# One-hots of the expert gate matrix laid out token by token, their matmuls one step later

## The chip, the cores and the metric

The kernel runs on one core of a Trainium2 chip. Its engines work side by side, each through its own list of instructions in order: TensorE (PE, with PEld for the loads of its stationary operand), VectorE (DVE), ScalarE (ACT), GpSimd (POOL) and SyncE (SP), which issues most of the DMAs. The metric is the device time of one execution in microseconds (us). Over three runs of the kernel before it was 1341.74 to 1342.67, with a median of 1341.83.

## What is computed

The reference is two transformer blocks over 256 tokens of width 1024: a block with window attention, retention and a gated feed-forward, then a block with a gated mixer, banded attention and a "PEER" feed-forward. The change lies in the PEER part, cut here to its core:

```python
q = (xb @ w_query).reshape(T, 8, 2, 128)
sc = jnp.einsum('thpd,hpkd->thpk', q, sub_keys)        # 8 heads, 2 halves, 128 keys each
s_top, i_top = lax.top_k(sc, 16)
cand = s_top[:, :, 0, :, None] + s_top[:, :, 1, None, :]
best, pos = lax.top_k(cand.reshape(T, 8, 256), 16)     # 16 experts of 128*128 per head
g = jax.nn.softmax(best, axis=-1)
h = jax.nn.gelu(jnp.einsum('thkd,td->thk', expert_u[eidx], xb))
out = jnp.einsum('thk,thkd->td', g * h, expert_v[eidx])
```

Each token so chooses 8 x 16 = 128 experts, each named by two numbers below 128, with a gate weight each.

## The kernel before, in words

The kernel gathers no experts. It computes the first layer for all 16384 of them, multiplies by a gate matrix that is zero where an expert was not chosen, and runs the whole second layer.

Every large product is made in fp32r from two parts of each operand (`hi`, a rounded copy, and `lo`, the rest): `mm3` (L105) issues three matmuls for each block of 128 along the sum, at L107, L108 and L109. A **unit** (L76) is one weight block of 128 x 1024: a DMA of 512 KB (L89), the copy to `whi` on ACT (L94) and the subtraction to `wlo` on DVE (L95). Units are given priority, so that they are issued some 80 instructions ahead of where the program stands; beyond that, the order on each engine is that of the program. There are three buffers for `whi` and `wlo` in this part of the kernel.

The first layer runs over j = 0 to 127 (L945). Each j takes one unit of `peer_u` and 24 matmuls of 256 columns (L926). After an odd j, the two results are passed through gelu into S, a matrix of 128 x 128 experts x 256 tokens (L932 to L936). Early in the loop DVE finds the top 16s and decodes the expert numbers; from then on `combine` (L851 to L879) is called after each odd j, about twice, until all 256 tokens are done near j = 115.

One call of `combine` makes the gate matrices of four tokens. The 128 chosen experts of a token lie along the partitions. A and B are one-hots of the experts' two numbers, and G0 and G1 are B times the gate's high and low half; all are fp16. The gate matrix of a token is then the product of A and G0 plus that of A and G1, 128 x 128 each, summed in PSUM (C). Its columns are one matmul each: eight matmuls of 128 columns for four tokens (L872), with a load of the stationary operand before each. DVE then multiplies S by C where S is already there (L875), and ACT copies C into the rest of S (L878).

A, B, G0 and G1 are stored as 128 numbers x 4 tokens with the token innermost. So DVE makes each for four tokens in one instruction of 512 elements (L861, L867, L868), and ACT makes G0 in four instructions, one for each token, since the gate is a factor per partition (L865). What a matmul reads for one token are 128 fp16 values that lie 8 bytes apart.

After the loop the second layer runs over 128 units of `peer_v` with 12 matmuls of 512 columns each (L974).

Of the kernel before, what the change touches and what calls it, by code (L numbers as in the profile page):

```python
# [7 lines left out]
F32 = mybir.dt.float32  # L8
F32R = mybir.dt.float32r
F16 = mybir.dt.float16  # L10
I32 = mybir.dt.int32
U32 = mybir.dt.uint32
AF = mybir.ActivationFunctionType
# [9 lines left out]
GP = 115  # L23
# [5 lines left out]
T = 256  # L29
# [13 lines left out]
class Net:  # L43
# [68 lines left out]
        return hl[0][:, k, ts], hl[1][:, k, ts]  # L112

    def gemm_t(self, ps, src, hl, K, k0=0, first=True, last=True, parts=None, engine=None):
        """ps[n, t] += W[k, n] x[k, t] for one unit of up to 8 k."""
        hi, lo = parts or self.unit(src, K * 128, engine=engine)
        for k in range(K):
            s = slice(k * 128, k * 128 + 128)
            self.mm3(ps, (hi[:, s], lo[:, s]), self.acts(hl, k0 + k),
                     first and k == 0, last and k == K - 1)  # L120
# [5 lines left out]
            self.mm3(ps, (hi[:, s], lo[:, s]), self.acts(hl, k), first and k == ks[0], last and k == ks[-1])  # L126

    def gemm_t_late(self, jobs, hl):
        """gemm_t of several (ps, src), with the last k after all others."""
        parts = [self.unit(src, 1024) for _, src in jobs]  # L130
        for (ps, _), w in zip(jobs, parts):
            self.gemm_k(ps, w, hl, range(7), first=True)
        for (ps, _), w in zip(jobs, parts):
            self.gemm_k(ps, w, hl, [7], last=True)

    def gemm_n(self, src, hl):
        """two banks, one per 128 tokens, of [t, 512] for a chunk of 512 columns."""
        banks = [self.mm_bank() for _ in range(2)]
        for q in range(4):
            hi, lo = self.unit(src[q], 1024)  # L140
            for tb in range(2):
                for k in range(2):
                    s = slice(k * 512, k * 512 + 512)
                    self.mm3(banks[tb], self.acts(hl, 2 * q + k, slice(tb * 128, tb * 128 + 128)),
                             (hi[:, s], lo[:, s]), q == 0 and k == 0, q == 3 and k == 1)
        return banks
# [8 lines left out]
            nc.vector.scalar_tensor_tensor(lo, src, scale, hi.bitcast(F32), op0=OP.mult, op1=OP.subtract)  # L155

    def rsqrt(self, y, ss, n, scale, pool=None):
        """y = (ss * scale + eps)^-1/2, all [128, n]."""
        nc = self.nc
        pool = pool or self.tiny  # L160
        v = pool.tile([128, n], F32, tag="nv", name="nv")
        nc.vector.tensor_scalar(v, ss, scale, EPS, op0=OP.mult, op1=OP.add)
        s = pool.tile([128, n], I32, tag="ns", name="ns")
        nc.vector.tensor_scalar(s, v.bitcast(I32), 1, None, op0=OP.logical_shift_right)
        nc.vector.tensor_scalar(y.bitcast(I32), s, -1.0, float(0x5F3759DF), op0=OP.mult, op1=OP.add)
        t = pool.tile([128, n], F32, tag="nt", name="nt")
        for _ in range(3):
            nc.vector.scalar_tensor_tensor(t, y, -0.5, y, op0=OP.mult, op1=OP.mult)
            nc.vector.tensor_tensor(out=t, in0=t, in1=v, op=OP.mult)
            nc.vector.scalar_tensor_tensor(y, t, 1.5, y, op0=OP.add, op1=OP.mult)  # L170
# [8 lines left out]
        nc.vector.tensor_tensor(out=acc, in0=acc, in1=sq, op=OP.add)  # L179

    def token_sums(self, acc):
        """[128 t, 2] from [128 d, 256 t] summed over d."""
        ps = self.ax_bank()
        for tb in range(2):
            self.nc.tensor.matmul(ps[:, tb:tb + 1], lhsT=acc[:, tb * 128:tb * 128 + 128],
                                  rhs=self.ones[:, 0:1], start=True, stop=True)
        return ps[:, 0:2]

    def rows(self, r, name):
        """[128, 256] with r of token t in column t, in every partition."""  # L190
        nc = self.nc
        ps = self.ax_bank()
        for tb in range(2):
            dg = self.work.tile([128, 128], F32, name="dg")
            nc.scalar.activation(dg, self.ident, AF.Copy, scale=r[:, tb:tb + 1])
            nc.tensor.matmul(ps[:, tb * 128:tb * 128 + 128], lhsT=self.ones, rhs=dg, start=True, stop=True)
        out = self.work.tile([128, T], F32, tag="rows", name=name)
        nc.scalar.activation(out, ps[:, :T], AF.Copy)
        return out
# [31 lines left out]
    def block1(self, actp):  # L231
        nc, a, tc = self.nc, self.a, self.tc
        mult, add, sub = OP.mult, OP.add, OP.subtract
        with ExitStack():
# [13 lines left out]
                    nc.scalar.activation(h[0][:, k], x0[:, k], AF.Copy, scale=g)  # L248
                nc.vector.scalar_tensor_tensor(h[1][:, k], x0[:, k], g, h[0][:, k].bitcast(F32), op0=mult, op1=sub)  # L249
            self.ident = self.load_const(self.const, "ident", [128, 128])  # L250
            self.iota16 = self.const.tile([128, 128, 4], F16, name="iota16")
            nc.sync.dma_start(out=self.iota16, in_=a["iota16"])

            with ExitStack() as s1:
                p = self.pool("mix", 1, s1)
# [446 lines left out]
    def peer(self, st, x3, h, acc):  # L702
# [145 lines left out]
        done = 0  # L848
        S, cp, ga = None, None, None

        def combine(jd):  # L851
            nonlocal done
            t0 = done
            A = cp.tile([128, 128, 4], F16, name="A", bufs=2)
            B = cp.tile([128, 128, 4], F16, name="B", bufs=2)
            G = [cp.tile([128, 128, 4], F16, name=f"G{i}", bufs=2) for i in range(2)]

            def spread(i):
                return gs[:, i, None, t0:t0 + 4].to_broadcast([128, 128, 4])

            nc.vector.tensor_tensor(out=B, in0=self.iota16, in1=spread(3), op=OP.is_equal)  # L861
            for i in range(2):
                if i == 0:
                    for t in range(4):
                        nc.scalar.activation(G[0][:, :, t], B[:, :, t], AF.Copy, scale=ga[:, t0 + t:t0 + t + 1])  # L865
                else:
                    nc.vector.tensor_tensor(out=G[i], in0=B, in1=spread(i), op=mult)  # L867
            nc.vector.tensor_tensor(out=A, in0=self.iota16, in1=spread(2), op=OP.is_equal)  # L868
            C = self.ax_bank()
            for t in range(4):  # L870
                for i in range(2):
                    nc.tensor.matmul(C[:, t * 128:t * 128 + 128], lhsT=A[:, :, t], rhs=G[i][:, :, t], start=i == 0,  # L872
                                     stop=i == 1)
            C = C.rearrange("p (t j) -> p j t", t=4)
            nc.vector.scalar_tensor_tensor(S[:, :jd, t0:t0 + 4], C[:, :jd], 1.0 / GSCALE, S[:, :jd, t0:t0 + 4],  # L875
                                           op0=mult, op1=mult)
            if jd < 128:
                nc.scalar.activation(S[:, jd:, t0:t0 + 4], C[:, jd:], AF.Copy, scale=1.0 / GSCALE)  # L878
            done += 4  # L879
# [41 lines left out]
        def first_layer(j):  # L921
            nonlocal pair
            e = j % 2
            if e == 0:
                pair = self.mm_bank()
            self.gemm_t(pair[:, e * T:e * T + T], a["peer_u"][j], xb, 8)  # L926
            if e == 0:
                return
            js = slice(j - 1, j + 1)
            p3 = pair.rearrange("p (e t) -> p e t", e=2)  # L930
            if done:
                gt = cp.tile([128, 2, T], F32, name="gt", bufs=2)  # L932
                nc.scalar.activation(gt[:, :, :done], p3[:, :, :done], AF.Gelu_apprx_tanh)
                nc.vector.tensor_tensor(out=S[:, js, :done], in0=S[:, js, :done], in1=gt[:, :, :done], op=mult)
            if done < T:
                nc.scalar.activation(S[:, js, done:], p3[:, :, done:], AF.Gelu_apprx_tanh)  # L936
# [8 lines left out]
        for j in range(128):  # L945
            first_layer(j)
            if c < 16 and j % QE == QE - 1:
                query(c)
                c += 1
                pump(PQ)  # L950
            elif c == 16 and last:
                score(*last)
                last = None
            if not ready:
                ready = pump(PU)
                if ready:
                    start = j
                    with tc.using_default_side("right"):
                        cp = self.pool("comb", 1, groups)
                    ga = cp.tile([128, T], F32, name="ga")  # L960
                    nc.scalar.activation(ga, gs[:, 0], AF.Copy)
            elif j % 2:
                while done < T and done * (GP - start) < T * (j - start):
                    combine(j + 1)
        while done < T:
            combine(128)
# [32 lines left out]


def wt(w, ks=None):
    """[n chunk][128 k][k chunk * 128 n]"""
    K, N = w.shape
    return w.reshape(K // 128, 128, N // 128, 128).transpose(2, 1, 0, 3).reshape(N // 128, 128, K)


def wn(w):
    """[n chunk of 512][pair of k chunks][128 k][2 * 512 n]"""
    K, N = w.shape
    return w.reshape(K // 256, 2, 128, N // 512, 512).transpose(3, 0, 2, 1, 4).reshape(N // 512, K // 256, 128, 1024)  # L1010

# [5 lines left out]
def layout(i):  # L1017
# [24 lines left out]
    dist = ii + 128 - jj  # L1042
    out["att_mask"] = np.where((dist >= 0) & (dist < 128), -dist, NEG).astype(np.float32)
    out["ident"] = np.eye(128, dtype=np.float32)
    out["iota16"] = np.tile(np.repeat(np.arange(128, dtype=np.float16), 4).reshape(128, 4), (128, 1, 1))
    out["w_q"] = wt(f["peer_w_query_2"][0])
    out["keys"] = f["peer_sub_keys_2"][0].transpose(0, 3, 1, 2)
    out["peer_u"] = f["peer_u_2"][0].reshape(128, 128, 8, 128).transpose(1, 3, 2, 0).reshape(128, 128, 1024)
# [37 lines left out]
```

## Time and profile before

| what | value |
|---|---|
| median of three timed runs | 1341.83 us |
| span of the profiled execution, first to last instruction | 1343.6 us |
| PE busy | 1334.3 us (99%) |
| DVE busy | 935.0 us (70%) |
| ACT busy | 768.4 us (57%) |
| share of the chain that ended last: L974 | 26% |
| share of that chain: L107, L108, L109 together | 63% |
| share of that chain: L872 | 5% |

The profiled execution has no time of its own beside its span, which is 1.8 us (0.1%) above the median of the timed runs. Times within a profile are counted from the span's start. Matmuls overlap: the duration of one, some 280 ns, is longer than the distance from one start to the next, so the pace of PE is read from counts per stretch of time and not from durations. DVE and ACT instructions overlap too, by some tens of ns.

### The profile page before, as it was taken

How to read it: one execution, taken by the hardware profiler on the slowest of the kernel's cores; microseconds unless marked ns; L12 is line 12 of the kernel's file. 1: busy time of each engine (PE TensorE's matmuls, PEld its weight loads, DVE VectorE, ACT ScalarE, POOL GpSimd, SP SyncE). 2: the span in 40 equal slices, each digit the busy share in tenths (PEclk: the TensorE clock that was granted, in tenths of full speed). 3: DMA queues.
4: the chain of work that ended last, by engine and by line, in shares of the span. 5: the costliest groups of instructions: out<-in, count | busy, mean ns of one | idle time of the engine just before them, and what ended most of it. 6: DMA issues, size and time to landing. Idle time of an engine off the chain costs nothing.

```text
span 1343.6 us, 24086 instructions
## 1 busy us (share of the span) xinstructions
PE 1334.3 (99%) x9384; PEld 1245.0 (93%) x9384; DVE 935.0 (70%) x1826; ACT 768.4 (57%) x1306; POOL 9.7 (1%) x12
## 2 busy tenths in 40 slices
PE   8999999999999999999999999999999999999998
PEld 8878999999998899999999999999998888888887
DVE  6767576766666977966996667777656666665665
ACT  5456445544455766444458887776555555555553
POOL 2000000000000000000000000000000000000000
PEclk8999999999999999999999999999999999999999
DMA  8545666666566446656564444444576666666664
GB/s 267 179 137 159 187 179 185 186 189 181 176 192 228 142 138 181 191 180 184 151 197 147 142 141 137 140 137 139 157 219 190 192 198 191 194 195 191 196 194 126
DMA packets 67633, 236.27 MB, mean 176 GB/s; under 512 B 7616, under 2 KB 9536, under 8 KB 67392
## 3 DMA queue, kind: packets, MB, share of 16 engines
q1 hardware_dynamic: 66512, 233.14, 57.1%
q8 instruction: 73, 1.20, 0.4%
q10 hardware_dynamic: 1008, 1.61, 0.3%
q14 instruction: 40, 0.33, 0.1%
HBM read 232.62 MB, written 2.10 MB: 175 GB/s over the span
## 4 chain that ended last, share of the span: by engine, by line
PE 95%; DVE 2%; DMA 1%; issue 0%; ACT 0%; POOL 0%; SPq 0%; ACTq 0%; POOLq 0%; DVEq 0%
PE ax L974 26%; PE mm L107 21%; PE mm L109 21%; PE mm L108 21%; PE ax L872 5%; DVE wlo L95 1%; DMA raw<-in_w_in_a_dram 1%; PE ax L837 0%; DMA xT<-in_xT_dram 0%; ACT whi L94 0%; PE ax L663 0%; PE ax L698 0%; PE ax L464 0%; PE ax L452 0%; PE ax L685 0%
## 5 line engine op out<-in xcount | busy, mean ns | idle before, releaser
L95 DVE TENSOR_TENSOR wlo<-raw,whi 128x1024 fp32r<-128x1024 f32 (+2 forms) x433 | 524.5, 1213 | 225.9 <-ACT whi L94 224.8
L94 ACT ACTIVATE whi<-raw 128x1024 fp32r<-128x1024 f32 (+3 forms) x439 | 458.0, 1046 | 332.9 <-PE mm L108 249.0
L107 PE MATMUL mm<-xbh,whi 128*128 128x256 f32 x1104 | 316.2, 287 | 0.0
L109 PE MATMUL mm<-xbh,wlo 128*128 128x256 f32 x1104 | 312.4, 283 | 0.8 <-DVE wlo L95 0.7
L108 PE MATMUL mm<-xbl,whi 128*128 128x256 f32 x1104 | 312.1, 283 | 0.0
L107 PE MATMUL mm<-acth,whi 128*128 128x256 f32 x848 | 241.0, 284 | 1.7 <-ACT acth L248 1.0
L108 PE MATMUL mm<-actl,whi 128*128 128x256 f32 x848 | 239.7, 283 | 0.7 <-DVE actl L249 0.7
L109 PE MATMUL mm<-acth,wlo 128*128 128x256 f32 x848 | 239.6, 283 | 0.0
L109 PEld LDWEIGHTS mm<-xbh,wlo 128*128 128x128 f32 x1104 | 210.6, 191 | 1.3 <-DVE wlo L95 1.2
L107 PEld LDWEIGHTS mm<-xbh,whi 128*128 128x128 f32 x1104 | 211.2, 191 | 0.2
L108 PEld LDWEIGHTS mm<-xbl,whi 128*128 128x128 f32 x1104 | 210.8, 191 | 0.0
L107 PEld LDWEIGHTS mm<-acth,whi 128*128 128x128 f32 x848 | 161.3, 190 | 2.8 <-ACT acth L248 1.2
L108 PEld LDWEIGHTS mm<-actl,whi 128*128 128x128 f32 x848 | 161.2, 190 | 1.6 <-DVE actl L249 1.6
L109 PEld LDWEIGHTS mm<-acth,wlo 128*128 128x128 f32 x848 | 161.3, 190 | 0.2 <-DVE wlo L95 0.2
L974 PE MATMUL ax<-wlo,keys 128*128 128x512 f32 x512 | 158.0, 389 | 0.0
L974 PE MATMUL ax<-whi,q 128*128 128x512 f32 x512 | 158.0, 389 | 0.0
L974 PE MATMUL ax<-whi,keys 128*128 128x512 f32 x512 | 157.9, 389 | 0.0
L151 ACT ACTIVATE keys<-S 128x256 fp32r<-128x256 f32 x128 | 53.4, 418 | 151.5 <-PE ax L974 151.5
L974 PEld LDWEIGHTS ax<-whi,q 128*128 128x128 f32 x512 | 96.1, 188 | 20.0
L974 PEld LDWEIGHTS ax<-wlo,keys 128*128 128x128 f32 x512 | 96.1, 188 | 19.9
L974 PEld LDWEIGHTS ax<-whi,keys 128*128 128x128 f32 x512 | 96.1, 188 | 19.8
L865 ACT ACTIVATE G<-B,ga 128x128 f16<-128x128 f16 x256 | 98.0, 575 | 0.0
(277 smaller groups left out, 1468.7 us busy)
## 6 DMA issues: line engine op xcount, KB each, us to landing
raw<-in_peer_u_dram SPq DMA_DIRECT2D x128, 512.0 KB, 3.6
raw<-in_peer_v_dram SPq DMA_DIRECT2D x128, 512.0 KB, 4.2
raw<-in_w_in_b_dram SPq DMA_DIRECT2D x32, 512.0 KB, 4.3
raw<-in_w_in_a_dram SPq DMA_DIRECT2D x31, 512.0 KB, 3.9
raw<-in_w_gate_dram SPq DMA_DIRECT2D x22, 512.0 KB, 3.6
raw<-in_w_up_dram SPq DMA_DIRECT2D x22, 512.0 KB, 3.7
raw<-in_w_out_dram SPq DMA_DIRECT2D x16, 512.0 KB, 4.3
raw<-in_w_down_dram SPq DMA_DIRECT2D x16, 512.0 KB, 3.6
```

The lines of the kernel that those rows point to most:

```text
L94: self.last_copy = nc.scalar.activation(hi[:, s], raw[:, s], AF.Copy).ins
L95: (engine or nc.vector).tensor_tensor(out=lo[:, s], in0=raw[:, s], in1=hi[:, s].bitcast(F32), op=OP.subtract)
L107: mm(ps, lhsT=left[0], rhs=right[0], start=first, stop=False)
L108: mm(ps, lhsT=left[0], rhs=right[1], start=False, stop=False)
L109: mm(ps, lhsT=left[1], rhs=right[0], start=False, stop=last)
L151: nc.scalar.activation(hi, src, AF.Copy)
L865: nc.scalar.activation(G[0][:, :, t], B[:, :, t], AF.Copy, scale=ga[:, t0 + t:t0 + t + 1])
L872: nc.tensor.matmul(C[:, t * 128:t * 128 + 128], lhsT=A[:, :, t], rhs=G[i][:, :, t], start=i == 0, stop=i == 1)
L974: nc.tensor.matmul(banks[tb][d], lhsT=s[left][:, ts], rhs=w[right][:, d * 512:d * 512 + 512], start=first, stop=end)
```

## The change

The four arrays of one-hots are now stored with the token outermost (4 tokens x 128 numbers), so that a matmul reads 128 adjacent fp16 values. DVE still makes A, B and G1 for four tokens in one instruction. To do so it reads the row of numbers 0 to 127 again for each token, and the expert numbers (and gate halves) from a new array `spread`, in which each value stands four times in a row; ACT makes it four times in all, for 64 tokens each. The function `form` makes the arrays; `combine` first forms the next four tokens and then issues the matmuls of the four formed a call earlier, so the first call issues none and a last one forms none. B and `gt` have one buffer in place of two. The constant `iota16` becomes 192 values per partition in place of 512. Comments were taken out of some helpers, which moves line numbers: L861, L865, L867, L868, L872, L875 and L878 become L874, L876, L878, L877, L893, L896 and L899.

```diff
-            self.iota16 = self.const.tile([128, 128, 4], F16, name="iota16")
-            nc.sync.dma_start(out=self.iota16, in_=a["iota16"])
+            both = self.const.tile([128, 192], F16, name="iota16")
+            nc.sync.dma_start(out=both, in_=a["iota16"])
+            self.iota = both[:, :128]
+            self.iota16 = both[:, 128:].rearrange("p (a q) -> p a q", q=4)
...
+        def form():
+            nonlocal made, spread
+            t0 = made
+            if t0 % 64 == 0:
+                spread = cp.tile([128, 3, 64, 4], F16, name="spread", bufs=2)
+                nc.scalar.activation(spread, gs[:, 1:4, t0:t0 + 64, None].to_broadcast([128, 3, 64, 4]), AF.Copy)
+            A = cp.tile([128, 4, 128], F16, name="A", bufs=2)
+            B = cp.tile([128, 4, 128], F16, name="B")
+            G = [cp.tile([128, 4, 128], F16, name=f"G{i}", bufs=2) for i in range(2)]
+            def four(x):
+                return x.rearrange("p t (r q) -> p t r q", q=4)
+            def each(i):
+                return spread[:, i - 1, t0 % 64:t0 % 64 + 4, None, :].to_broadcast([128, 4, 32, 4])
+            numbers = self.iota.rearrange("p (r q) -> p r q", q=4)[:, None].to_broadcast([128, 4, 32, 4])
+            nc.vector.tensor_tensor(out=four(B), in0=numbers, in1=each(3), op=OP.is_equal)
+            for t in range(4):
+                nc.scalar.activation(G[0][:, t], B[:, t], AF.Copy, scale=ga[:, t0 + t:t0 + t + 1])
+            nc.vector.tensor_tensor(out=four(A), in0=numbers, in1=each(2), op=OP.is_equal)
+            nc.vector.tensor_tensor(out=four(G[1]), in0=four(B), in1=each(1), op=mult)
+            formed.append((A, G))
+            made += 4
...
         def combine(jd):
             nonlocal done
+            if made < T:
+                form()
+            if len(formed) < 2 and made < T:
+                return
             t0 = done
-            A = cp.tile([128, 128, 4], F16, name="A", bufs=2)
-            B = cp.tile([128, 128, 4], F16, name="B", bufs=2)
...
+            A, G = formed.pop(0)
             C = self.ax_bank()
             for t in range(4):
                 for i in range(2):
-                    nc.tensor.matmul(C[:, t * 128:t * 128 + 128], lhsT=A[:, :, t], rhs=G[i][:, :, t], start=i == 0,
+                    nc.tensor.matmul(C[:, t * 128:t * 128 + 128], lhsT=A[:, t], rhs=G[i][:, t], start=i == 0,
                                      stop=i == 1)
...
-                gt = cp.tile([128, 2, T], F32, name="gt", bufs=2)
+                gt = cp.tile([128, 2, T], F32, name="gt")
...
-                while done < T and done * (GP - start) < T * (j - start):
+                while done < T and (done + len(formed) * 4) * (GP - start) < T * (j - start):
```

On PE the order hardly changes: after every second unit stand two groups of eight matmuls, as before; in the first such place there is now one group. On DVE the rows of one pair of j (two units, two calls) before are these. The number behind a name tells one use of a tile from the next; `wlo` is the subtraction for a unit, S with `gt` the multiplication by gelu, S with `ax` the multiplication by the gate matrix.

```order
L861 TENSOR_TENSOR B_9010<-iota16_139,gs_5868 128x512
L95 TENSOR_TENSOR wlo_8977<-raw_8975,whi_8976 128x1024
L861 TENSOR_TENSOR B_9032<-iota16_139,gs_5868 128x512
L867 TENSOR_TENSOR G1_9012<-B_9010,gs_5868 128x512
L868 TENSOR_TENSOR A_9009<-iota16_139,gs_5868 128x512
L934 TENSOR_TENSOR S_6217<-S_6217,gt_8896 128x2x24
L95 TENSOR_TENSOR wlo_9056<-raw_9054,whi_9055 128x1024
L875 SCALAR_TENSOR_TENSOR S_6217<-ax_8911,S_6217 128x58x4
L875 SCALAR_TENSOR_TENSOR S_6217<-ax_8933,S_6217 128x58x4
L867 TENSOR_TENSOR G1_9034<-B_9032,gs_5868 128x512
L868 TENSOR_TENSOR A_9031<-iota16_139,gs_5868 128x512
```

Now the rows of a pair are these, on the same engine:

```order
L874 TENSOR_TENSOR B_9001<-iota16_139,spread_8573 128x512
L877 TENSOR_TENSOR A_9000<-iota16_139,spread_8573 128x512
L878 TENSOR_TENSOR G1_9003<-B_9001,spread_8573 128x512
L95 TENSOR_TENSOR wlo_9077<-raw_9075,whi_9076 128x1024
L874 TENSOR_TENSOR B_9023<-iota16_139,spread_8573 128x512
L877 TENSOR_TENSOR A_9022<-iota16_139,spread_8573 128x512
L878 TENSOR_TENSOR G1_9025<-B_9023,spread_8573 128x512
L955 TENSOR_TENSOR S_6217<-S_6217,gt_8996 128x2x28
L95 TENSOR_TENSOR wlo_9156<-raw_9154,whi_9155 128x1024
L896 SCALAR_TENSOR_TENSOR S_6217<-ax_9011,S_6217 128x60x4
L896 SCALAR_TENSOR_TENSOR S_6217<-ax_9033,S_6217 128x60x4
```

The same instructions stand there in the same number, with the three of one call now together; B_9023 overwrites the one buffer of B, which ACT must have read for G0 by then.

On ACT a pair before reads:

```order
L94 ACTIVATE whi_9055<-raw_9054 128x1024
L933 ACTIVATE gt_8896<-mm_8835 128x2x24
L936 ACTIVATE S_6217<-mm_8835 128x2x232
L865 ACTIVATE G0_9011<-B_9010,ga_8509 128x128 x4
L865 ACTIVATE G0_9033<-B_9032,ga_8509 128x128 x2
L878 ACTIVATE S_6217<-ax_8911 128x70x4
L878 ACTIVATE S_6217<-ax_8933 128x70x4
L865 ACTIVATE G0_9033<-B_9032,ga_8509 128x128
L94 ACTIVATE whi_9085<-raw_9084 128x1024
L865 ACTIVATE G0_9033<-B_9032,ga_8509 128x128
```

And now:

```order
L94 ACTIVATE whi_9046<-raw_9045 128x1024
L954 ACTIVATE gt_8887<-mm_8826 128x2x20
L957 ACTIVATE S_6217<-mm_8826 128x2x236
L876 ACTIVATE G0_8915<-B_8914,ga_8509 128x128 x4
L899 ACTIVATE S_6217<-ax_8902 128x70x4
L899 ACTIVATE S_6217<-ax_8924 128x70x4
L876 ACTIVATE G0_9002<-B_9001,ga_8509 128x128
L94 ACTIVATE whi_9076<-raw_9075 128x1024
L876 ACTIVATE G0_9002<-B_9001,ga_8509 128x128 x3
```

Three of the four readers of B_9001 now stand behind the copy whi_9076, and the overwriting of B comes behind them.

## Rows read from the trace of the kernel before

**Rows 1.** The page, sections 1 and 2: busy time, granted TensorE clock in 40 slices.

```profile
PE 1334.3 (99%) x9384; PEld 1245.0 (93%) x9384; DVE 935.0 (70%) x1826; ACT 768.4 (57%) x1306; POOL 9.7 (1%) x12
...
PEclk8999999999999999999999999999999999999999
```

**Rows 2.** The page, section 4: chain that ended last, shares by line.

```profile
PE ax L974 26%; PE mm L107 21%; PE mm L109 21%; PE mm L108 21%; PE ax L872 5%; DVE wlo L95 1%; DMA raw<-in_w_in_a_dram 1%; PE ax L837 0%; DMA xT<-in_xT_dram 0%; ACT whi L94 0%; PE ax L663 0%; PE ax L698 0%; PE ax L464 0%; PE ax L452 0%; PE ax L685 0%
```

**Rows 3.** Busy time by stretches: us, PE, PEld, DVE, ACT, POOL, clock, DMA share, GB/s.

```profile
200.00:300.00 100.00, 100.00 (x846) 100.00 (x845) 71.10 (x112) 52.63 (x83) 0.00 (x0) 1.00 0.62 186
550.00:600.00 50.00, 50.00 (x421) 50.00 (x420) 40.74 (x164) 23.24 (x30) 0.00 (x0) 1.00 0.60 185
...
1000.00:1100.00 100.00, 100.00 (x443) 82.84 (x442) 60.76 (x74) 54.15 (x74) 0.00 (x0) 1.00 0.64 197
```

**Rows 4.** Pieces of that chain in order of time: start us, us, what.

```profile
462.70 1.90 PE ax L597 x32
...
645.75 0.45 PE ax L837 x4
...
712.10 1.89 PE ax L872 x16
719.74 1.91 PE ax L872 x16
```

**Rows 5.** Line L872: ns min/median/max, first and last start; who waited for it.

```profile
L872 PEld LDWEIGHTS <-A x512: 110/117/136, 711.9 to 956.5; 128*128 128x128 f16 x171
L872 PE MATMUL ax<-G,A x512: 283/297/304, 711.9 to 956.6; 128*128 128x128 f16 x171
...
  DVE G L867: 45.8, 32
```

**Rows 6.** Groups by shape, loads of stationary operands: busy us, mean ns, idle before.

```profile
L837 PEld LDWEIGHTS ax<-keys,qT 128*128 128x128 f32 x64 | 8.6, 191 | 0.0
...
L597 PEld LDWEIGHTS ax<-wsT,gv 128*64 128x64 f32 x32 | 1.7, 137 | 0.1
```

**Rows 7.** Groups by shape, on DVE and ACT.

```profile
L94 ACT ACTIVATE whi<-raw 128x1024 fp32r<-128x1024 f32 x423 | 447.3, 1060 | 324.6 <-PE mm L108 240.9 <-issue 39.8 <-PE mm L109 25.8
...
L865 ACT ACTIVATE G<-B,ga 128x128 f16<-128x128 f16 x256 | 98.0, 575 | 0.0
...
L867 DVE TENSOR_TENSOR G<-B,gs 128x512 f16<-128x512 f16 x64 | 27.0, 421 | 45.8 <-PE ax L872 45.8
...
L781 DVE TENSOR_TENSOR oh<-iota,dec 128x1024 f16<-128x1024 f16 x8 | 5.4, 686 | 0.0
...
L934 DVE TENSOR_TENSOR S<-S,gt 128x512 f32<-128x512 f32 x6 | 4.1, 685 | 0.0
```

**Rows 8.** Line L195, ACT with a factor per partition: ns min/median/max.

```profile
L195 ACT ACTIVATE dg<-ident,rac x2: 387/394/402, 24.6 to 24.9; 128x128 f32<-128x128 f32 x2
```

**Rows 9.** DVE timeline early and late: start, us, instruction, idle before and releaser.

```profile
759.02 0.43 DVE L867 TENSOR_TENSOR G<-B,gs 128x512 f16<-128x512 f16 x1 [1.30 <-PE ax L872]
759.36 0.42 DVE L868 TENSOR_TENSOR A<-iota,gs 128x512 f16<-128x512 f16 x1
...
759.87 1.22 DVE L95 TENSOR_TENSOR wlo<-raw,whi 128x1024 fp32r<-128x1024 f32 x1
761.00 0.75 DVE L875 SCALAR_TENSOR_TENSOR S<-ax,S 128x256 f32<-128x256 f32 x2
...
763.80 1.23 DVE L95 TENSOR_TENSOR wlo<-raw,whi 128x1024 fp32r<-128x1024 f32 x1 [1.05 <-ACT whi L94]
...
941.63 0.43 DVE L867 TENSOR_TENSOR G<-B,gs 128x512 f16<-128x512 f16 x1 [1.30 <-PE ax L872]
...
946.43 1.23 DVE L95 TENSOR_TENSOR wlo<-raw,whi 128x1024 fp32r<-128x1024 f32 x1 [0.27 <-ACT whi L94]
```

**Rows 10.** Waits from 700 to 960 us: us in total, times, longest.

```profile
ACT whi L94 <- PE mm L108: 39.0, 35, 1.9
...
DVE B L861 <- ACT G L865: 0.6, 1, 0.6
```

More of the change, by code (lines that the diff above doesn't have):

```diff
@@ L849, in peer @@
         S, cp, ga = None, None, None
+        made = 0
+        spread, formed = None, []
+        def form():
[19 more added lines that the diff above has]
+            made += 4
@@ L851, in combine @@
         def combine(jd):
             nonlocal done
+            if made < T:
+                form()
+            if len(formed) < 2 and made < T:
+                return
             t0 = done
-            A = cp.tile([128, 128, 4], F16, name="A", bufs=2)
-            B = cp.tile([128, 128, 4], F16, name="B", bufs=2)
-            G = [cp.tile([128, 128, 4], F16, name=f"G{i}", bufs=2) for i in range(2)]
-            def spread(i):
-                return gs[:, i, None, t0:t0 + 4].to_broadcast([128, 128, 4])
@@ L861, in combine @@
[L861 to L868, printed above, removed]
+            A, G = formed.pop(0)
@@ L1044, in layout @@
     out["ident"] = np.eye(128, dtype=np.float32)
-    out["iota16"] = np.tile(np.repeat(np.arange(128, dtype=np.float16), 4).reshape(128, 4), (128, 1, 1))
+    out["iota16"] = np.tile(np.concatenate([np.arange(128), np.repeat(np.arange(16), 4)]).astype(np.float16), (128, 1))
     out["w_q"] = wt(f["peer_w_query_2"][0])
```

## The prediction, made before the change was run

> **What bounds the kernel now.** I read the page first: PE is busy for 99% of the span at the full granted clock [rows 1], and the chain that ended last lies on PE almost from end to end, with 5% of it on L872, the matmuls of the gate matrix [rows 2]. So only what shortens PE's list, or makes PE wait, can show. Then the stretches of time [rows 3], for the pace: 846 matmuls of 256 columns in 100 us are 118.2 ns each, 443 of 512 columns are 225.7 ns each. The difference, 107.5 ns for 256 columns, is 0.42 ns a column; 118.2 - 107.5 leaves 10.7 ns that each matmul costs beside its columns. Then the pieces of the chain around L872 [rows 4]: sixteen take 1.90 us, 118.75 ns each, and the next sixteen come 7.64 us later. A pair of j is so 48 x 118.2 = 5.67 us for two units, 1.90 us for two groups of gate matmuls, and 0.07 us of rest. The reader is to see that a gate matmul of 128 columns takes as long as one of 256. Something makes it twice as slow as its columns are many; its operands are read 8 bytes apart.
>
> The line's own view [rows 5] says that nobody on PE's path waits there: the 45.8 us that DVE waits for L872 are DVE's slack.
>
> **PE's matmuls.** 512 gate matmuls stay, each with its load. What changes is the pace. Adjacent values should stream at 0.42 ns a column: 128 x 0.42 + 10.7 = 64.4 ns. Before: 512 x 118.75 = 60.8 us. After: 512 x 64.4 = 33.0 us. Saved: 27.8 us, 0.87 us a pair.
>
> No row shows an fp16 matmul with adjacent operands, so this price has bounds. From below: the columns alone, 53.75 ns, save 33.3 us; L597, 128 columns of f32 with loads of 64 columns, goes at 1.90 / 32 = 59.4 ns [rows 4] and would save 30.4 us. From above: L837, 128 columns of f32 with loads of 128, goes at 0.45 / 4 = 112.5 ns [rows 4] and would save 3.2 us. Slower than 8 bytes apart it can hardly become, as nothing is added to what is read; 0 is the upper end. I take 64.4, since it is what the present 118.75 becomes if the strided stream is the whole reason: 256 columns' worth plus the same 10.7.
>
> Which of the two operands is slow? The load takes 117 ns in fp16 [rows 5], against 191 for 128 columns of f32 and 137 for 64, and those of 137 keep up with a pace of 59.4 [rows 4, 6]. So the fp16 load, strided as it is, should keep up with a pace below 60, and the moving operand is left as the slow one.
>
> [...]
>
> **DVE.** The same instructions, six one-hots a pair. An early pair has 1.30 + 1.05 us of idle time in 7.64, so 5.3 us of work; a late one 1.30 + 0.27, so 6.1 us [rows 9]. Against a pair of 6.77 us, 1.5 and 0.7 us stay idle. That is thinner cover, not a bound. It holds if the new pattern, runs of four values with a repeat between, costs the 421 ns of now; L781 reads both inputs in just such runs, 1024 values in 686 ns, 0.52 ns for each value more, so it should [rows 7]. If they fell to the f32 rate, 685 ns for 512, six times 0.265 us = 1.6 us would come on top: 6.9 to 7.7 us a pair, DVE would lead with 7.3 on the mean, and of the 27.8 us some 11 would be left (1331).
>
> The wait that DVE has for L872 (G1 before, A now) stays: with two buffers it holds until PE has reached the group of the pair. What queues behind it are gelu's multiplication and the `wlo` of a unit that PE needs two units, 5.7 us, later. The new wait is B's: one buffer, to be read by four G0 on ACT. Between two B stand A, G1 and a `wlo`, 0.34 + 0.34 + 1.13 us from start to start [rows 9]. ACT needs four G0 and, behind the first, a unit copy. That copy starts when PE frees a buffer, and DVE's `wlo` needs the same copy, so both wait for the same event and B should come free before DVE is there. I take 0; the price without that cover is the third rival.
>
> **ACT and the rest.** G0 goes from 575 ns toward the 391 of L195, the same size with adjacent values [rows 7, 8]: 8 x 0.18 = 1.5 us a pair off an engine that waits 39.0 us for PE here [rows 10]; 0 on the path. The four `spread` of 768 values cost at most six L195 each, 2.3 us, 9.4 in all, within those 39.0; 0. With one `gt`, gelu waits for a multiplication of nearly a pair ago; 0. DMA: two units of 512 KB in 6.77 us are 155 GB/s, where the stretch at 550 us gets 185 [rows 3]; 0. The last group moves to j = 117, and ten units, 28 us of PE, still stand before the second layer; 0. The smaller constant saves 80 KB, 0.4 us at 186 GB/s, early on another queue position that nobody on the chain waits for; between 0 and 0.4 us gained, I take 0.
>
> The sum: 27.8 us off the profiled span, 1343.6 to 1315.8. The timed median lies 1.8 us below that span, so 1341.83 - 27.8 = 1314.0.
>
> **Rivals.** *The load is partly exposed.* A faster stream leaves less time to hide it. Loads of 64 and 128 columns of f32 differ by 54 ns, so 83 of the 137 are latency [rows 6], and the fp16 load has 117 - 83 = 34 ns of its own. Were those added to each matmul: 64.4 + 34 = 98 ns, saving 10.6 us: 1331. Against it: the matmuls of 256 columns hide a longer load almost wholly.
>
> *No change: the load sets the pace.* 118.75 is near L837's 112.5, which has the same 128 columns to load. If a load takes that long whatever its type and layout, the gate matmuls stay as they are: 1341.8. For it: the coincidence of 118.75 with 118.2, two layouts with one pace. Against it: the 117 and 191 of the loads.
>
> *Slower: B's single buffer.* DVE stands at B until ACT has done a unit copy (1.06 us [rows 7]) and four G0 at 0.39, 2.6 us a pair with nothing beside it. 5.7 + 2.6 = 8.3 us a pair on DVE against 7.64 now: 32 x 0.66 = 21 us more, 1363, the gain on PE being lost in waits for `wlo`. It decides from an uncovered wait of 7.64 - 5.7 = 1.9 us a pair. For it: three G0 stand behind a copy in the new order. Against it: DVE's `wlo` stands before that B and needs the same copy; in the kernel before, B waited for G0 once, 0.6 us [rows 10].
>
> **Chances.** The forecast 0.66, the exposed load, or a DVE that leads in part, 0.14, no change 0.12, slower 0.08. A change of 0.2%, 2.7 us, is about what can be told from none. So faster 0.80, same 0.12, slower 0.08. The forecast's own range is 1308 to 1320 (53 to 76 ns a matmul); with the first rival's it is 1307 to 1333, which holds about 8 in 10.
>
> **What would show it.** Sixteen gate matmuls in 1.0 us on the chain and pairs 6.8 us apart; PE at 99% and the full clock; about 420 ns for the one-hots on DVE with 0.7 us or more of idle time a pair; G0 near 390 ns; from 960 us on everything as before, 28 us earlier. Sixteen in 1.9 us would mean that the stride was not the reason. PE idle before L109 with `wlo` as releaser would mean that DVE or the wait for B leads.

## The result, and the profile after

The changed kernel takes 1311.42 us (1310.85 to 1312.15, four runs) where the kernel before takes 1342.05 beside it: a ratio of 0.9764 with an interval of 0.975 to 0.9778. The forecast was 1314.0 with a range of 1307 to 1333. Direction and mechanism came out as forecast; the gain, 30.6 us, is 2.8 us larger than the sum.

The page of the changed kernel, busy times (section 1) and the chain by line (section 4), as in [rows 1, 2]:

```profile
PE 1299.7 (99%) x9384; PEld 1211.2 (92%) x9384; DVE 936.9 (72%) x1826; ACT 758.1 (58%) x1311; POOL 9.4 (1%) x12
...
PE ax L995 27%; PE mm L107 22%; PE mm L108 21%; PE mm L109 21%; PE ax L893 2%; DVE wlo L95 1%; PE ax L839 1%; DMA raw<-in_w_in_a_dram 0%; ACT whi L94 0%; PE ax L665 0%; PE ax L700 0%; PE ax L466 0%; PE ax L454 0%; PE ax L687 0%; DVE ns L164 0%
```

PE is still the chain. The gate matmuls, L893 now, fell from 5% of it to 2%; the shares of the other large lines moved by at most a point.

Pieces of that chain in order of time (start us, us, what), as in [rows 4]; L185 ends the second block's mixer, L839 is the last scoring of keys, L995 the second layer:

```profile
506.34 0.34 PE ax L185 x4
...
641.77 0.45 PE ax L839 x4
...
714.38 0.91 PE ax L893 x16
721.09 0.91 PE ax L893 x16
...
957.40 347.52 PE ax L995 x1533
```

And the same landmarks in the trace of the kernel before:

```profile
510.14 0.34 PE ax L185 x4
...
645.75 0.45 PE ax L837 x4
...
991.45 347.52 PE ax L974 x1533
```

Sixteen gate matmuls take 0.91 us where they took 1.90, and the next sixteen follow 6.71 us later where it was 7.64. A good ruler for all that follows is the stretch from the last scoring to the start of the second layer, which holds all that the change touches but the load of the smaller constant at the start: 345.70 us before (645.75 to 991.45), 315.63 now (641.77 to 957.40), 30.07 less. In runs whose gate stage should not differ it agrees within 0.05 us (`e0`, `e4`, `e6` and `e8` with the changed kernel, `e5` with the kernel before). The second layer takes 347.52 us in both.

The two profiled spans differ by 34.1 us, more than the stretch: this profile of the kernel before is 3.8 us late already at L185, ahead of the whole PEER part. A kernel with the old gate matmuls (`e5_delay_only` below) has that landmark at 506.40, another (`e2_g_strided`) at 511.53, and the times of the kernel before beside the experiments reach from 1341.55 to 1347.3 us. Part of the lateness is the pace of the matmuls there: from 200 to 300 us the kernel before has 846 of them at the full clock [rows 3], the changed kernel 855, although up to there the programs differ only in the size of one constant:

```profile
200.00:300.00 100.00, 100.00 (x855) 100.00 (x854) 71.02 (x112) 53.17 (x82) 0.00 (x0) 1.00 0.62 187
```

So gains below are read from the stretch, not from the spans. Beside the experiments the kernel before took 1344.77 to 1345.21 us on the median, and the timed gain was 33.6 to 34.2 us (`e0`, `e4`, `e6`, `e8`), 3 to 4 more than the stretch. What varies ahead of L185, and whether the change has a part in it, stays open.

The groups by shape (busy us, mean ns, idle before and its releaser), answering to [rows 5, 7], and the waits from 700 to 960 us (total, times, longest), answering to [rows 10]:

```profile
L876 ACT ACTIVATE G<-B,ga 128x128 f16<-128x128 f16 x256 | 82.5, 394 | 0.0
...
L893 PEld LDWEIGHTS <-A 128*128 128x128 f16 x512 | 28.7, 98 | 1.5
...
L877 DVE TENSOR_TENSOR A<-iota,spread 128x512 f16<-128x512 f16 x64 | 26.9, 421 | 22.8 <-PE ax L893 22.8
...
L862 ACT ACTIVATE spread<-gs 128x768 f16<-128x768 f16 x4 | 3.4, 840 | 0.0
```

```profile
ACT whi L94 <- PE mm L108: 38.2, 43, 1.9
DVE wlo L95 <- ACT whi L94: 32.2, 37, 1.7
DVE A L877 <- PE ax L893: 22.8, 32, 1.1
ACT S L899 <- DVE S L896: 15.4, 27, 0.9
```

G0 costs 394 ns where it cost 575, a one-hot 421 as before. No row names PE as the one that waits. DVE's wait for the gate matmuls halved, 45.8 to 22.8 us: this is where the shorter pairs took from its slack, while its wait for `whi` grew from 23.9 to 32.2. ACT has a new wait for DVE, 15.4 us, of which nothing reaches PE.

### The profile page after: what moved, and what is told of

The parts are those of the page before. It is cut to its first block, busy times and chain, and to the rows that moved or that the text cites. A ratio compares the mean times of both kernels' runs of the same rounds, so it can differ in the third digit from the quotient of the medians.

```text
span 1309.5 us, 24136 instructions
## 1 busy us (share of the span) xinstructions
PE 1299.7 (99%) x9384; PEld 1211.2 (92%) x9384; DVE 936.9 (72%) x1826; ACT 758.1 (58%) x1311; POOL 9.4 (1%) x12
## 4 chain that ended last, share of the span: by engine, by line
PE 96%; DVE 3%; ACT 0%; DMA 0%; issue 0%; SPq 0%; DVEq 0%; ACTq 0%
PE ax L995 27%; PE mm L107 22%; PE mm L108 21%; PE mm L109 21%; PE ax L893 2%; DVE wlo L95 1%; PE ax L839 1%; DMA raw<-in_w_in_a_dram 0%; ACT whi L94 0%; PE ax L665 0%; PE ax L700 0%; PE ax L466 0%; PE ax L454 0%; PE ax L687 0%; DVE ns L164 0%
## 5 line engine op out<-in xcount | busy, mean ns | idle before, releaser
L995 PE MATMUL ax<-whi,keys 128*128 128x512 f32 x512 | 158.0, 389 | 0.0
L995 PE MATMUL ax<-whi,q 128*128 128x512 f32 x512 | 157.9, 389 | 0.0
L995 PE MATMUL ax<-wlo,keys 128*128 128x512 f32 x512 | 157.9, 389 | 0.0
L995 PEld LDWEIGHTS ax<-wlo,keys 128*128 128x128 f32 x512 | 96.1, 188 | 20.0
L995 PEld LDWEIGHTS ax<-whi,keys 128*128 128x128 f32 x512 | 96.0, 188 | 20.0
L995 PEld LDWEIGHTS ax<-whi,q 128*128 128x128 f32 x512 | 96.1, 188 | 19.9
L152 DVE TENSOR_TENSOR q<-S,keys 128x256 fp32r<-128x256 f32 x128 | 54.3, 425 | 49.7 <-ACT keys L151 49.7
```

The lines of the kernel that those rows point to most:

```text
L152: nc.vector.tensor_tensor(out=lo, in0=src, in1=hi.bitcast(F32), op=OP.subtract)
L995: nc.tensor.matmul(banks[tb][d], lhsT=s[left][:, ts], rhs=w[right][:, d * 512:d * 512 + 512], start=first, stop=end)
```

## The experiments

**Which operand.** `e1_a_strided` keeps only the stationary operand as before, `e2_g_strided` only the moving one:

```diff
# e1_a_strided
-            A = cp.tile([128, 4, 128], F16, name="A", bufs=2)
+            A = cp.tile([128, 128, 4], F16, name="A", bufs=2)
-                    nc.tensor.matmul(..., lhsT=A[:, t], rhs=G[i][:, t], ...)
+                    nc.tensor.matmul(..., lhsT=A[:, :, t], rhs=G[i][:, t], ...)
# e2_g_strided
-            B = cp.tile([128, 4, 128], F16, name="B")
+            B = cp.tile([128, 128, 4], F16, name="B")
+            (G0 and G1 the same way)
-                    nc.tensor.matmul(..., lhsT=A[:, t], rhs=G[i][:, t], ...)
+                    nc.tensor.matmul(..., lhsT=A[:, t], rhs=G[i][:, :, t], ...)
```

In both, the operands of the old form are made as before the change, from the old row of numbers beside the new one (640 values in place of 192).

Expected of the first:

> The changed kernel, with only the stationary operand A stored as before (token innermost, values 8 bytes apart); B, G0 and G1 stay token by token. Theory M (the moving operand's stride made the matmuls slow): sixteen gate matmuls in 0.9 to 1.0 us on the chain, 57 to 62 ns each, time 1311 to 1314 us. Theory S (the stationary operand's load was slow): sixteen in 1.9 us, 1341 to 1343 us. If both have a part: between, near 1327.

Expected of the second:

> The mirror image: A token by token, B, G0 and G1 stored as before (8 bytes apart). Theory M: sixteen gate matmuls in 1.9 us, 118 ns each, 1341 to 1343 us, and G0 on ScalarE back at 575 ns. Theory S: sixteen in 0.9 us, 1311 to 1313 us.

Measured, from the chain (the last scoring, a group, the second layer) and then the groups by shape of `e1_a_strided`:

```profile
642.94 0.45 PE ax L839 x4
...
735.77 0.93 PE ax L893 x16
...
959.28 347.52 PE ax L995 x1533
```

```profile
L893 PEld LDWEIGHTS <-A 128*128 128x128 f16 x512 | 29.7, 114 | 1.5
```

and from the chain of `e2_g_strided`:

```profile
647.13 0.45 PE ax L839 x4
...
735.40 1.86 PE ax L893 x16
743.01 1.85 PE ax L893 x16
...
991.54 347.52 PE ax L995 x1533
```

With A strided, 1314.0 us, ratio 0.9774 (0.9758 to 0.9789), stretch 316.34. With G strided, 1344.14 us, ratio 0.9993 (0.9982 to 1.0003), stretch 344.41. So theory M holds: 29.36 us of the 30.07 come without any change to A, and giving B, G0 and G1 their old layout back takes 28.78 of them away (344.41 - 315.63). The load of the strided A takes 114 ns in place of 98, and 0.71 us in all reaches the stretch, 1.4 ns a matmul. In `e2_g_strided` the load of the adjacent A takes 115 ns on the median: the length of a load on record follows the slow stream too. G0 is back at 573 ns there.

**How far apart.** `e3_pairs` stores pairs of tokens, so that what a matmul reads lies 4 bytes apart:

```diff
-            A = cp.tile([128, 4, 128], F16, name="A", bufs=2)
+            A = cp.tile([128, 2, 128, 2], F16, name="A", bufs=2)
+            (B, G0 and G1 the same way)
-                    nc.tensor.matmul(..., lhsT=A[:, t], rhs=G[i][:, t], ...)
+                    nc.tensor.matmul(..., lhsT=A[:, t // 2, :, t % 2], rhs=G[i][:, t // 2, :, t % 2], ...)
```

DVE makes the pairs straight from the expert numbers, without `spread`.

> All four arrays stored in pairs of tokens: what a matmul reads lies 4 bytes apart, in place of 2 (changed kernel) or 8 (before). Theory P (two values within 8 bytes are enough for the full pace): sixteen gate matmuls in 0.9 us, 1311 to 1313 us. Rival (anything but adjacent fp16 values halves the pace): sixteen in 1.9 us, 1341 to 1343 us. A price that grows with the stride: near 1.4 us and 1327.

Measured: 1313.72 us, ratio 0.977 (0.9755 to 0.9785), stretch 316.52, and on the chain

```profile
734.43 0.94 PE ax L893 x16
```

So theory P fits: at 4 bytes the pace is 58.8 ns, at 2 bytes 56.9, at 8 bytes 116 to 119. It is no price that grows with the stride, nor one of anything that isn't adjacent. Somewhere between 4 and 8 bytes the pace halves. That two values within 8 bytes are what is wanted is a reading that fits; it isn't shown, as other strides weren't tried.

**The step's delay.** `e4_same_step` issues the matmuls in the call that forms their operands; `e5_delay_only` adds the delay alone to the kernel before:

```diff
# e4_same_step
-            if len(formed) < 2 and made < T:
-                return
...
# e5_delay_only (on the kernel before; the lines that make the arrays go into form())
+            if made < T:
+                form()
+            if len(formed) < 2 and made < T:
+                return
+            A, G = formed.pop(0)
```

> The changed kernel with the matmuls issued in the call that forms their operands, as before the change. Theory (the delay by a step does nothing, since A and G stand ready long before PE is there): 1310.5 to 1312.5 us, no wait of PE for A or G. Rival (the step keeps PE from waiting now that pairs are shorter): PE waits for G0 or G1 in most pairs, 0.1 to 0.5 us each, 1314 to 1327 us.

> The kernel before with only the delay: the matmuls issued one call later, the arrays still with the token innermost. Theory (the delay does nothing): within 2 us of the kernel before, ratio 0.998 to 1.002, sixteen gate matmuls in 1.9 us. Rival (the delay itself gives a part of the gain): 1330 to 1338 us where the kernel before has 1342.

Measured: 1311.27 us, ratio 0.9752 (0.9738 to 0.9765), stretch 315.59; and 1344.66 us, ratio 0.9996 (0.9986 to 1.0005), stretch 345.66. The delay does nothing in either layout.

**B's single buffer.** `e6_two_b` gives B two buffers (`bufs=2`).

> The changed kernel with two buffers for B in place of one. Theory (the wait for B's single buffer is covered): the time of the changed kernel, 1310.5 to 1313 us, and VectorE's idle time only moves to another wait. Rival (B's wait takes something): 1 to 4 us less than the changed kernel.

Measured: 1311.5 us, ratio 0.9755 (0.9741 to 0.9769), stretch 315.63. The wait is covered, as reckoned; among the waits of the changed kernel from 700 to 960 us there is none of B for G0.

**The price of a matmul beside its columns.** `e7_half_cols` cuts each gate matmul into two of 64 columns, each with its load:

```diff
-                for i in range(2):
-                    nc.tensor.matmul(C[:, t * 128:t * 128 + 128], lhsT=A[:, t], rhs=G[i][:, t], ...)
+                for u in range(4):
+                    i = u % 2
+                    s = slice(u // 2 * 64, u // 2 * 64 + 64)
+                    nc.tensor.matmul(C[:, t * 128:t * 128 + 128][:, s], lhsT=A[:, t], rhs=G[i][:, t, s], ...)
```

> The changed kernel with each gate matmul cut into two of 64 columns, with a load of 128 columns before each: 1024 matmuls in place of 512, the same columns in sum. Theory C (56.9 ns is 53.3 for the columns and a constant of 3.6 for each fp16 matmul, loads hidden): 30 ns each, 32 of them in 0.97 us where 16 took 0.91, and 1313 to 1314 us. Rival L (the fp16 load has 34 ns of its own and sets the pace once the stream is shorter): 34 to 38 ns each, 32 in 1.1 to 1.2 us, 1317 to 1321 us. Rival F (a load with its matmul can't go faster than some 55 ns): 32 in 1.8 us, 1340 us.

Measured: 1314.26 us, ratio 0.9774 (0.9758 to 0.979), stretch 317.82, and on the chain

```profile
729.69 0.95 PE ax L895 x32
736.46 0.95 PE ax L895 x32
```

29.7 ns each, theory C: 64 columns more cost 56.9 - 29.7 = 27.2 ns, 0.42 a column (54.4 for 128), and 2.5 ns stand beside them, where theory C had put 53.3 and 3.6. The trace has all 1024 loads, with a median of 98 ns. So an fp16 load of 128 columns fits behind 29.7 ns and doesn't set the 56.9 of the changed kernel. Four loads in a row are of the same A here, where the changed kernel has two; whether 29.7 ns would do with new values each time isn't shown.

`e10_f32r_halves` puts the other ruler to the test: the first layer's fp32r matmuls, for j below 32, in halves of 128 columns with an f32 load each:

```diff
-            self.gemm_t(pair[:, e * T:e * T + T], a["peer_u"][j], xb, 8)
+            if j < 32:
+                w = self.unit(a["peer_u"][j], 1024)
+                for u in range(2):
+                    us = slice(u * 128, u * 128 + 128)
+                    for k in range(8):
+                        s = slice(k * 128, k * 128 + 128)
+                        self.mm3(pair[:, e * T:e * T + T][:, us], (w[0][:, s], w[1][:, s]), self.acts(xb, k, us),
+                                 k == 0, k == 7)
+            else:
...
```

> The changed kernel with the first-layer matmuls of j = 0 to 31 cut in two halves of 128 columns, each with its own f32 load: 48 in place of 24 for each of 32 j. Theory L (the f32 load of 128 columns has a floor near 113 ns, so what the f32r matmuls cost beside their columns says nothing on fp16): 112 to 120 ns for each of 128 columns, 32 x 24 x some 115 = 88 us more, near 1400 us. Rival (a constant of some 11 ns beside the columns for any matmul): 64 to 66 ns each, 768 x 11 = 9 us more, near 1320 us.

Measured: 1413.07 us in one run. Scorings of keys on its chain:

```profile
575.83 0.45 PE ax L839 x4
595.24 0.45 PE ax L839 x4
614.65 0.45 PE ax L839 x4
```

Between two of them stand the scoring, 144 half matmuls and 24 whole ones at 119.9 ns, so (19.41 - 0.45 - 2.88) / 144 = 111.7 ns for 128 columns. (The 119.9 come from the changed kernel, where two scorings, at 629.81 and 641.77 us, have 96 whole ones between.) Theory L holds: half the columns, nearly the same time. That the load sets it agrees with the loads at L185 in the kernel before, f32 of 128 columns in front of matmuls of a single column:

```profile
422.11 0.53 PEld L185 LDWEIGHTS ax<-ones,acg 128*128 128x128 f32 x4
```

One lasts 0.19 us, so they start (0.53 - 0.19) / 3 = 0.113 us apart. The halves make 80 of the 102 us. Some 15 of the others were lost between 519 and 556 us, 1.3 of them in waits and the rest to TensorE's clock: from the scoring at 518.84 to that at 575.83 us pass 57.0 us, in the changed kernel 27.4 (518.69 to 546.09), and six halved j account for 14.9 of the difference. The last 7 came near 750 us. Both are told at the end.

**How much VectorE can still take.** `e8_one_more` makes A twice in each call, `e9_three_more` A, B and G1:

```diff
             nc.vector.tensor_tensor(out=four(A), in0=numbers, in1=each(2), op=OP.is_equal)
+            nc.vector.tensor_tensor(out=four(A), in0=numbers, in1=each(2), op=OP.is_equal)
```

> The changed kernel with one one-hot (A) made twice by VectorE in each call: two instructions of 0.34 us more a pair of j. Theory (VectorE has 1.5 us to spare early and 0.7 us late in a pair of 6.71 us): 0 to 2 us above the changed kernel, VectorE's wait for the gate matmuls shrinks from 22 us to a few. Rival (VectorE already leads in part of the stretch, the pairs follow its work): 32 pairs by 0.3 to 0.68 us, 1321 to 1333 us.

> The changed kernel with A, B and G1 each made twice by VectorE: six instructions of 0.34 us, 2.0 us more a pair, 7.3 us of work early and 8.1 late against pairs of 6.71. Theory (VectorE leads from about 1 us a pair on): pairs of 7.3 to 8.1 us on the chain, TensorE waiting for wlo, about 32 x 1.0 us more: 1335 to 1347 us. Rival (the scheduler and the three unit buffers hide more): under 1325 us.

Measured: 1311.19 us, ratio 0.9754 (0.9741 to 0.9767), stretch 315.63, for one more; 1330.26 us, ratio 0.9895 (0.988 to 0.991), stretch 334.44, for three. The waits from 700 to 960 us of `e8_one_more`:

```profile
DVE wlo L95 <- ACT whi L94: 20.1, 17, 1.7
DVE A L877 <- PE ax L894: 16.0, 26, 1.1
```

and of `e9_three_more`, with two late rows of its PE timeline after them:

```profile
PEld mm L109 <- DVE wlo L95: 11.5, 17, 1.0
PE mm L109 <- DVE wlo L95: 7.9, 16, 0.8
```

```profile
886.85 0.38 PE L109 MATMUL mm<-xbh,wlo 128*128 128x256 f32 x1 [0.56 <-DVE wlo L95]
894.60 0.38 PE L109 MATMUL mm<-xbh,wlo 128*128 128x256 f32 x1 [0.59 <-DVE wlo L95]
```

0.68 us more a pair disappears in DVE's slack, although its wait for the gate matmuls shrank only to 16.0 us and not to the few expected; its wait for `whi` shrank too, from 32.2 to 20.1. 2.04 us more makes PE wait for `wlo`, as the prediction said that a leading DVE would show, but the stretch grows by 18.8 us only, 0.59 a pair, and 1330 us lies between the theory's range and the rival's: late pairs are 7.75 us, not 8.1. DVE has no idle time from 850 to 900 us there, so its own work was 7.75 - 2.04 = 5.7 us late in the stretch, where I had reckoned 6.1; the idle times of [rows 9] were not all that a pair has.

**The changed kernel again**, as a measure for the runs beside it:

> The changed kernel once more, as a measure for the runs beside it: 1310 to 1314 us. For the stretch ahead of the first layer: if the 4 us by which the profile of the changed kernel was ahead of that of before at 506 us belong to one execution, this profile may lie anywhere from 506 to 511 us at that place; if they come with the change, at 506 us.

Measured: 1311.02 us, ratio 0.9757 (0.9742 to 0.9771), stretch 315.64, L185 at 505.93. Its place at L185 agrees with the first theory and with the second; `e5_delay_only`, with the old gate matmuls at 506.40, speaks for the first. No version here beats the changed kernel by more than its runs differ.

## Why the prediction was right

*PE bounds the kernel, and only the pace of the gate matmuls counts.* Right: 30.07 us in the stretch, 30.6 timed; the second layer is the same to 0.01 us.

*The moving operand's stride is the reason.* Right, by `e1` and `e2`. What the argument from the lengths of the loads concluded held: strided fp16 loads keep up with 58.1 ns (`e1`), adjacent ones with 29.7 (`e7`). The lengths themselves were weak evidence, as the 117 ns was partly the slow stream's (`e2`).

*64.4 ns a matmul.* This term was mis-sized: 56.9 measured. I had split 118.2 ns of the fp32r matmuls into columns and a constant of 10.7, and given the constant to fp16. `e7` shows 2.5 ns for fp16, and `e10` that an fp32r matmul with an f32 load of 128 columns costs 112 ns with half of its 256 columns, so a fit over 256 and 512 columns of them says nothing about a short fp16 one. The fit was unsteady too: with the 855 matmuls of the changed kernel in place of the 846, it would have given a constant of 8.2 and 62.6 ns. The strided 118.75, which seemed to carry the same constant, is 116 with the moving operand alone strided (`e2`); the stationary one's stride costs 1.4 (`e1`).

*The sum.* 512 x (118.75 - 56.9) = 31.7 us come off the gate matmuls, 3.9 more than forecast. The stretch gives 30.07, 1.6 us less. The rest of a pair, two units, went from 7.65 - 1.90 = 5.75 us (pairs on the mean of fifteen) to 6.71 - 0.91 = 5.80, 0.05 us for each of 32. PE's timeline places this at the seam behind a group, here before and then now:

```profile
765.51 2.05 PE L872 MATMUL ax<-G,A 128*128 128x128 f16 x16
...
767.52 0.28 PE L108 MATMUL mm<-xbl,whi 128*128 128x256 f32 x1
```

```profile
767.87 1.07 PE L893 MATMUL ax<-G,A 128*128 128x128 f16 x16
...
768.95 0.28 PE L108 MATMUL mm<-xbl,whi 128*128 128x256 f32 x1
```

From a group's first matmul to the second matmul behind it are 2.01 us before and 1.08 now, which is the whole difference of the pairs. With its share of the seam a gate matmul so became 0.94 us / 16 = 58.75 ns cheaper, from 118.75 to 60.0 where 64.4 was forecast. The term was wrong by 7.5 ns and the seam, which the sum left out, took 3.1 of them back; that the sum came out within 2.3 us is partly luck. Why the seam grew is open. That I set the gain against the profiled span, 1.8 us above the median, was a misreading too: a run's time lies 1.8 us above its own span (1311.29 against 1309.5), so the profiled execution of the kernel before was a long one, and the subtraction from the median alone was what counted.

*DVE, ACT and DMA at 0.* Right. One-hots cost 421 ns in the new pattern, G0 394 against 391 forecast, `spread` 840 ns against a bound of 2.3 us. DVE's cover was thinner than before and a little better than reckoned (`e8`, `e9`).

*The rivals.* The exposed load and no change are out by `e1` and `e7`, a DVE that leads in part by `e8`, B's single buffer by `e6`.

## What to carry to other kernels

When matmuls on a PE-bound path take twice as long as their columns, look at how far apart the moving operand's values lie before looking at its size: here 8 bytes doubled the time (116 ns against 56.9), 4 bytes did not (58.8), and the stationary operand's stride cost 1.4 ns. The engines that make the operand paid nothing for the better layout here, where DVE writes it in inner runs of four values (421 ns as before). And take the price of a matmul from one of the same type: the 10.7 ns fitted on matmuls with f32 loads were four times the 2.5 that fp16 showed.

## What the runs showed of the hardware that was not expected

In `e10_f32r_halves`, stretches as in [rows 3]:

```profile
519.00:525.00 6.00, 5.31 (x46) 5.10 (x45) 5.92 (x15) 4.38 (x10) 0.00 (x0) 1.00 0.74 232
525.00:530.00 5.00, 4.38 (x30) 4.10 (x30) 5.00 (x31) 0.81 (x2) 0.00 (x0) 0.83 0.37 105
530.00:535.00 5.00, 5.00 (x26) 5.00 (x25) 5.00 (x38) 1.06 (x1) 0.00 (x0) 0.50 0.01 3
...
550.00:555.00 5.00, 5.00 (x25) 5.00 (x25) 1.23 (x1) 1.06 (x1) 0.00 (x0) 0.50 0.03 6
555.00:560.00 5.00, 5.00 (x44) 5.00 (x44) 2.55 (x11) 2.06 (x4) 0.00 (x0) 0.94 0.48 143
560.00:565.00 5.00, 5.00 (x47) 5.00 (x47) 4.97 (x37) 1.54 (x2) 0.00 (x0) 1.00 0.24 93
```

And a piece of PE's timeline there (start us, us, instruction):

```profile
555.12 0.41 PE L108 MATMUL mm<-xbl,whi 128*128 128x256 f32 x1
555.33 0.41 PE L109 MATMUL mm<-xbh,wlo 128*128 128x256 f32 x1
555.54 0.31 PE L107 MATMUL mm<-xbh,whi 128*128 128x256 f32 x1
555.70 0.27 PE L108 MATMUL mm<-xbl,whi 128*128 128x256 f32 x1
555.81 0.28 PE L109 MATMUL mm<-xbh,wlo 128*128 128x256 f32 x1
```

From 519 to 530 us, where the halved matmuls start, PE is idle for 1.3 of 11 us, in waits of at most 0.7 us for its own operands. Then the granted clock falls to 0.50 and stays there until 555 us, although PE shows no idle time from 530 us on. Matmuls of 128 columns come every 0.21 us and not every 0.11, and so do the whole ones while the clock is low. The clock rises while PE works on 24 whole matmuls of 256 columns (0.94 from 555 to 560 us). After that the halved ones run at the full clock, 1.00, every 0.11 us. It falls once more between 745 and 760 us, behind the last of them: 0.79 there, with PE idle for 6.2 of the 15 us. In both kernels, `e8` and `e9`, where the matmuls are whole, the clock is 1.00 from 519 to 560 us; the changed kernel has, for one,

```profile
530.00:545.00 15.00, 15.00 (x128) 15.00 (x127) 15.00 (x77) 8.05 (x10) 0.00 (x0) 1.00 0.60 176
```

A PE that shows as busy without a gap (5.00 of 5.00 us at 0.50 here) is so no proof of the full clock; the PEclk row has to be read beside it. What in the halved matmuls kept the clock low there, and not later, wasn't tried.
